# Diffusion trunk on one core: folds issued three weight splits behind, a first weight moved ahead of reloads, background matmuls moved out of a norm

## The chip, the cores and the metric

The kernel runs on one core of a Trainium2 chip. The metric is the device time of one execution, in microseconds, and lower is better. A core has a matrix engine (TensorE, PE in the profile; PEld is its loading of stationary operands), VectorE (DVE), ScalarE (ACT), GpSimd (POOL) and SyncE (SP), which here issues nearly all transfers. Each engine works through its own instructions in the order in which the program was built, and semaphores make one wait for another.

## The reference

One step of a two-layer trunk over 1024 latent and 128 context tokens of width 1024, all in float32. What is computed, cut to what matters:

```python
for i in range(2):
    h = rmsnorm(x, norm_mix_g[i]) * (1 + sc1) + sh1          # sc, sh, gt = silu(c) @ w_mod[i] + b_mod[i]
    x = x + gt1 * (gla_mixer(h) if i == 0 else fourier_mixer(h))
    h = rmsnorm(x, norm_ffn_g[i]) * (1 + sc2) + sh2
    a, g = split(h @ w_up[i])                                 # 2 x 2816 columns
    x = x + gt2 * ((silu(dwconv3(a)) * g) @ w_down[i])        # "ConvGLU"
y = rmsnorm(x, final_norm_g)
```

The first mixer is gated linear attention with 4 heads, whose outputs go through one output product with `gla_w_o`. The second is a Fourier transform over tokens and channel groups, followed by an output product with `fnet_w_o`.

## The kernel before, in words

Every product is made of three matmuls (`mm3`, L94 to L99): each operand is split into a rounded high part, which ACT writes, and the remainder, which DVE or POOL makes by subtraction; the three matmuls are high by high (L97), high by low (L98) and low by high (L99). So each weight goes through a load into a raw tile (`wr`, two buffers), a high part on ACT and a low part on POOL or DVE (`split`, L83, and `weight`, L90; `wh`, six buffers).

The order of the work is not written out: a planner orders each engine's instructions at build time by priority, which is program order, by when operands are ready in its own model, and by free buffers. `tc.high_priority()` moves a block's priority forward, `later(n)` moves it back by n, and `tc.issue_after(ins)` puts the instructions of a block that run on the engine of `ins` behind `ins` in that engine's order, without a wait.

Three places are touched.

**The down product of the ConvGLU** (`ffn`, L979) runs in both layers. It is organised as a one-level fast multiplication: nine steps, the first five of them `a2`, `s1`, `s4`, `a1`, `s2` (`steps`, L1088), each over 11 pairs j of hidden tiles. For each j a step needs the stationary weight of that j, split by `stationary` (L1068: the high part on ACT, L1073, the low part on DVE, L1074), and the moving activations, loaded and split by `moving` (L1077: `hr` loaded by SP, `hh` on ACT, L1083, and `hl` on DVE, L1084, in two pieces of 288 columns; the tiles for them hold two j at a time). Then PE runs 24 matmuls of 288 columns. Steps `s1` and `s4` use sums of weights, which `fold` (L1061) makes in place on DVE (L1064): one fold for each j in `s1`, two in `s4`, each on 128 x 512 elements (the last j has half-width pieces). Before, all folds of a step are placed behind one and the same instruction: `behind` (L1126), the low part that was last traced for the kind of weight that goes before:

```python
if j == 0 and what in ("s1", "s4"):
    behind = made[{"s1": 1, "s4": 2}[what]].ins
```

Step `s2` also folds one weight for each j, after the moving part and with no such edge. The results of a step are added into the residual pages by DVE (L1165).

**The output product of the attention** (`w_out`, L611) multiplies the heads' outputs with `gla_w_o`. Outputs of the first three heads were stored to memory and are loaded again and split by `load_ot` (L604) through the same two raw tiles. For the first two heads `load_ot(0, 1)` stands at L665, before the last head's loop over token groups. `w_out((0, 1), X)` (L675) comes inside that loop, set back by `LV` = 300; it loads its four weights itself, each followed by six blocks of 12 matmuls of 384 columns. Each block ends in an addition on DVE (L624) into one of four pages that `load_x` (L309) has just filled with the residual; even and odd blocks use different pages. A block's result waits in one of three PSUM tiles.

**The Fourier layer and the norm after it.** The modulation vectors of the second ConvGLU are made in small background matmuls (`mod_background`, L150, its matmuls L175 and L186), a generator that `tick` (L193) advances. Its 24 groups are spread by hand: two ticks at each of eight token folds (L1246), two before the time transform of the second pair of channel groups (L1305), two after the output product (L1388), and the rest with `finish()` (L1420) in the midst of the norm of the second ConvGLU, between the variance part of `rstd_steps` (L256) and its broadcast (L273). The ConvGLU's first up-product begins with small weight tiles from `ffn_first_weights` (L864, split by `ffn_split`, L806, here in two halves of 512 columns at L808 and L809), which are traced after that norm, at high priority.

Of the kernel before, what the change touches and what calls it, by code (L numbers as in the profile page):

```python
# [15 lines left out]
F32 = mybir.dt.float32  # L16
# [4 lines left out]
ALU = mybir.AluOpType  # L21
# [10 lines left out]
NCH = 3  # L32
# [13 lines left out]
def trunk(tc, a, o):  # L46
# [43 lines left out]
    def weight(src, n, name, eng=None):  # L90
        with tc.high_priority():
            return split(raw_w(src, n, name), n, name, eng)
# [100 lines left out]
    def tick(n=1, behind=None):  # L193

        for _ in range(n):
            while queue:
                try:
                    with tc.issue_after(behind.ins) if behind else ExitStack():
                        next(queue[0])
                    break  # L200
                except StopIteration:
                    queue.pop(0)

    def finish():
        while queue:
            tick()
# [397 lines left out]
    def load_ot(*hs):  # L604
        for cg, h in ((cg, h) for cg in range(3) for h in hs):
            raw = sb.tile([P, 1032], F32, tag="wr", bufs=2, name="otr")[:, :2 * CH].rearrange("p (d t) -> p d t", d=2)
            nc.sync.dma_start(raw, ot_dram[h][:, :, cols(cg)].rearrange("d p t -> p d t"))
            for d in range(2):
                split_ot(h, d, cg, raw[:, d])

    def w_out(hs, X, after=None):  # L611
        gate = vec(0, 2)
        nk = 2 * len(hs)

        def block(m, ch, whl, mi):
            ps = mm_ps(f"wo{ch}")
            for k in range(nk):
                q = (mi * nk + k) * P
                t = ots[hs[k // 2], k % 2]
                mm3(ps[:, :CH], [w[:, q:q + P] for w in whl],  # L620
                    (t[:, cols(ch)], t[:, T + ch * CH:T + (ch + 1) * CH]), k == 0, k == nk - 1)
            for s, c in parts(ch):
                x = X(m, ch)[:, s]
                V.scalar_tensor_tensor(x, ps[:, s], gate(m, c), x, op0=ALU.mult, op1=ALU.add)  # L624
        if not after:
            for m2 in range(4):
                whl = weight(a["gwo"][0, m2], 1024, f"wo0{m2}")
                for ch in range(NCH):
                    for mi in range(2):
                        block(2 * m2 + mi, ch, whl, mi)  # L630
            return
        ws = []
        for m2 in range(4):
            raw = raw_w(a["gwo"][1, m2], 1024, f"wo1{m2}")
            if m2 < 2:
                pg = page(f"wo1{m2}", F32R)
                whl = pg[:, :1024], pg[:, 1024:2048]
                S.activation(whl[0], raw[:, :1024], AF.Copy)
                G.tensor_tensor(whl[1], raw[:, :1024], whl[0].bitcast(F32), op=ALU.subtract)
                ws.append(whl)  # L640
            else:
                ws.append(split(raw, 1024, f"wo1{m2}"))
        for ch in range(NCH):
            for m in range(KT):
                block(m, ch, ws[m // 2], m % 2)
                feed(X(m, ch), m == 0, span(ch))
                after(m, ch)
# [5 lines left out]
    for h in range(H):  # L653
        with later(LR):
            gla_r(h, pages)
        att = attention(h, qk, pages)
        next(att)
        pages = {}
        if h < 3:
            with later(LQ):  # L660
                qk = gla_qk(h + 1)
                ahead = gla_gates_v(h + 1, pages)
        else:
            finish()
            load_ot(0, 1)  # L665
        for cg in range(3):
            next(att)
            if h < 3:
                with later(LV):
                    next(ahead)  # L670
            elif cg == 0:
                xp, X, Xw = xpages("x1")
                load_x(xp, a["xT"])
                with later(LV):
                    w_out((0, 1), X)  # L675
        for g in (att, ahead):
            for _ in g:
                pass
# [300 lines left out]
    def ffn(l, xp, rs, xd, after, ahead=None, w=None, stages=None):  # L979
# [83 lines left out]
            for (c, xx), (_, yy) in zip(wd[x, j], wd[y, j]):  # L1063
                V.tensor_tensor(xx, *((yy, xx) if reverse else (xx, yy)), op=op)  # L1064

        made = {}

        def stationary(kind, j, wt=None):  # L1068
            if wt is None:
                wt = sb.tile([P, 1032], F32R, tag="wh", bufs=6, name=f"wd{l}")[:, :1024]  # L1070
            for c, x in wd[kind, j]:
                hi, lo = wt[:, c], wt[:, 512:][:, c]
                S.activation(hi, x, AF.Copy)  # L1073
                made[kind] = V.tensor_tensor(lo, x, hi.bitcast(F32), op=ALU.subtract)  # L1074
            return wt

        def moving(name, ss, j):  # L1077
# [31 lines left out]
        for n, (what, name, kind, (mh, th), ss) in enumerate(steps):  # L1109
# [10 lines left out]
            for j in range(NP):  # L1120
                for load, *args in loads.get((n, j), ()):
                    load(*args)
                with tc.high_priority():

                    if j == 0 and what in ("s1", "s4"):
                        behind = made[{"s1": 1, "s4": 2}[what]].ins  # L1126

                    if what == "s1":
                        with tc.issue_after(behind):
                            fold(2, 3, ALU.add, j)  # L1130
                    elif what == "s4":
                        with tc.issue_after(behind):
                            fold(2, 0, ALU.subtract, j)
                            fold(1, 2, ALU.subtract, j)
                    wt = kept.get((what, j))
                    if wt is None or n < 7:
                        wt = stationary(kind, j, wt)
                    hi, lo = moving(name, ss, j)
                    if what == "s2":
                        fold(2, 3, ALU.subtract, j, reverse=True)  # L1140
                held.append((what, ss, wt, hi, lo, what in fresh and j == 0, j == NP - 1))

                if n < len(steps) - 1 or j != NP - 2:
                    for m in range(4):
                        for args in held:
                            products(m, *args)
                    held = []
                if n == 7 and j == 5:
                    norms = after(X, xp, rs, key(1, 0), key(0, 0))
                if n == 8 and j == 5:  # L1150
                    norms = after(X, xp, rs, key(1, 1))
                if n > 6 and j > 4 and j != 6 or n == 8 and j < 5:
                    next(norms, None)
# [110 lines left out]
    for pr_ in range(2):  # L1264
# [36 lines left out]
            i = (g * 2 + typ) * 4 + hl * 2 + half  # L1301
            return pq[i // 6][:, (i % 6) * CH:(i % 6 + 1) * CH]

        if pr_ == 1:
            tick(2)  # L1305
        t2 = weight(a["dft_t"][2][:, :512], 512, f"dt2{pr_}")
        for half in range(2):
            tw = weight(a["dft_t"][half], 1024, f"dt{half}{pr_}")
# [35 lines left out]
    for m in range(KT):  # L1344
# [40 lines left out]
        V.scalar_tensor_tensor(xc, ps2[:, 256:CH], gate(m, 1), xc, op0=ALU.mult, op1=ALU.add)  # L1385
        for ch in range(NCH):
            feed(X(m, ch), m == 0, span(ch))
    tick(2)  # L1388


    def final(X, xp, rs, *keys):
# [23 lines left out]
    xs = dr.tile([KT, P, T], F32, name="xs1")  # L1415
    save_x(xp, xs)
    rs = new_rs()
    norm = rstd_steps(rs, *map(span, range(NCH)))
    next(norm)
    finish()  # L1420
    for _ in norm:
        pass
    ffn(1, xp, rs, xs, final)
    ctx.close()


# [132 lines left out]
```

## Time and profile before

| what | value |
|---|---|
| median of 3 runs (lowest, highest) | 2590.62 us (2589.14, 2591.91) |
| profiled execution | 2588.23 us, its span 2586.4 us |
| mean granted TensorE clock | 0.977 of full speed |
| PE, PEld busy | 2429.6 us (94%), 2332.2 us (90%) |
| DVE, ACT, POOL busy | 1844.4 us (71%), 1090.3 us (42%), 732.9 us (28%) |
| mean transfer rate | 120 GB/s |

The profile shows one execution. Busy time of an engine leaves out waits; idle time is put down to the instruction that ended the wait. A matmul's record is longer than the step from one matmul to the next, as they are pipelined, so the rate of PE is best read from how many matmul records begin in a stretch. A granted clock of 1.00 is 2.4 GHz and one of 0.50 is 1.2 GHz; a value between them is a mix over the stretch.

### The profile page before, as it was taken

What the parts mean: (1) busy time and instruction counts of PE and PEld (TensorE: products, weight loads), DVE (VectorE), ACT (ScalarE), POOL (GpSimd) and SP (SyncE); (2) the same over time, 40 slices, a digit from 0 to 9 for tenths busy, and PEclk for the clock granted to TensorE, in tenths of its full rate; (3) what the DMA queues carried; (4) which work ended last, traced back from release to release, by engine and by line L of the source; (5) the groups of instructions that cost most, each with busy time, mean ns of one, the idle gap of its engine ahead of it and who ended that gap; (6) DMA issues with size and microseconds to landing.
All of it is one profiled execution on the core that took longest, in us unless ns stands there. A gap on an engine that the chain in (4) does not pass through costs nothing. (4 is left out here: it accounts for less than half of the span.)

```text
span 2586.4 us, 46546 instructions
## 1 busy us (share of the span) xinstructions
PE 2429.6 (94%) x18122; PEld 2332.2 (90%) x18122; DVE 1844.4 (71%) x3339; ACT 1090.3 (42%) x2086; POOL 732.9 (28%) x548
## 2 busy tenths in 40 slices
PE   6999999988999999999989998999899999998997
PEld 5998988887999899999989996998899999998997
DVE  7647384666698677777766877287987777787676
ACT  5435343444364233333335564344533333333453
POOL 3435344543103334344100005330144444410000
PEclk9999999998999999999999998999999999999999
DMA  7213222104334443323754347343223232375334
GB/s 261 74 48 93 81 88 79 54 21 145 109 108 126 155 137 99 114 82 101 242 178 134 113 153 214 102 166 134 94 79 115 82 114 82 98 240 176 93 84 126
DMA packets 200972, 309.85 MB, mean 120 GB/s; under 512 B 18288, under 2 KB 142064, under 8 KB 200752
## 3 DMA queue, kind: packets, MB, share of 16 engines
q1 hardware_dynamic: 196528, 302.66, 36.8%
q10 hardware_dynamic: 4224, 4.23, 0.5%
q8 instruction: 142, 2.33, 0.4%
q14 instruction: 78, 0.64, 0.1%
HBM read 233.71 MB, written 73.11 MB: 119 GB/s over the span
## 5 line engine op out<-in xcount | busy, mean ns | idle before, releaser
L98 PE MATMUL pd<-hl,wd 128*128 128x288 f32 x1112 | 331.9, 301 | 28.7 <-DVE hl L1084 28.5
L99 PE MATMUL pd<-hh,wd 128*128 128x288 f32 x1112 | 329.9, 300 | 0.0
L97 PE MATMUL pd<-hh,wd 128*128 128x288 f32 x1112 | 317.6, 299 | 5.5 <-ACT hh L1083 3.2
L98 PEld LDWEIGHTS pd<-hl,wd 128*128 128x128 f32 x1112 | 213.7, 192 | 31.2 <-DVE hl L1084 30.7
L809 POOL TENSOR_TENSOR s<-wa,s 128x512 fp32r<-128x512 f32 x114 | 157.3, 1380 | 278.4 <-ACT s L808 278.4
L1084 DVE TENSOR_TENSOR hl<-hr,hh 128x288 fp32r<-128x288 f32 x308 | 138.3, 454 | 133.8 <-ACT hh L1083 133.5
L1083 ACT ACTIVATE hh<-hr 128x288 fp32r<-128x288 f32 x308 | 133.4, 437 | 233.7 <-PE pd L98 218.8
L97 PEld LDWEIGHTS pd<-hh,wd 128*128 128x128 f32 x1112 | 205.6, 189 | 10.1 <-ACT hh L1083 5.3
L99 PEld LDWEIGHTS pd<-hh,wd 128*128 128x128 f32 x1112 | 213.1, 192 | 0.0
L809 POOL TENSOR_TENSOR a<-wa,a 128x512 fp32r<-128x512 f32 x76 | 100.0, 1316 | 332.4 <-ACT a L808 231.0
L808 ACT ACTIVATE s<-wa 128x512 fp32r<-128x512 f32 x120 | 75.5, 630 | 190.7 <-DVE wa L826 114.7
L977 ACT ACTIVATE hid<-hid 128x576 f32<-128x576 f32 x88 | 60.4, 686 | 157.1 <-DVE hid L972 100.5
L1074 DVE TENSOR_TENSOR wd<-wd,wd 128x512 fp32r<-128x512 f32 (+1 forms) x184 | 116.4, 642 | 9.9 <-ACT wd L1073 4.9
L1073 ACT ACTIVATE wd<-wd 128x512 fp32r<-128x512 f32 (+1 forms) x184 | 104.6, 580 | 26.7 <-DVE wd L1064 14.9
L808 ACT ACTIVATE a<-wa 128x512 fp32r<-128x512 f32 x80 | 50.4, 631 | 142.8 <-PE pa L99 75.9
L1209 POOL TENSOR_TENSOR fn<-fn 128x512 f32<-128x512 f32 x8 | 14.1, 1762 | 330.9 <-ACT wp L728 311.1
L860 DVE TENSOR_TENSOR q<-q,ps 128x288 f32<-128x288 f32 x232 | 98.5, 445 | 11.3 <-PE ps L99 9.7
L535 POOL TENSOR_TENSOR le<-vbr 128x384 f32<-128x384 f32 x72 | 74.3, 1036 | 109.3 <-PE lv L549 93.7
L97 PE MATMUL pa<-fh1x,a 128*128 128x288 f32 x320 | 95.4, 298 | 5.7 <-DVE c L860 3.3
L541 POOL TENSOR_TENSOR le<-le,qk 128x384 f32<-128x384 f32 x72 | 89.4, 1246 | 36.6 <-ACT le L540 35.1
L860 DVE TENSOR_TENSOR c<-q,pa 128x288 f32<-128x288 f32 x80 | 36.1, 451 | 87.7 <-PE pa L99 87.7
L97 PE MATMUL ps<-fh1x,s 128*128 128x288 f32 x320 | 95.2, 298 | 3.0 <-DVE hid L917 3.0
(689 smaller groups left out, 8917.3 us busy)
## 6 DMA issues: line engine op xcount, KB each, us to landing
hr<-hid SPq DMA_DIRECT2D x308, 144.0 KB, 2.2
wm<-in_wmod SPq DMA_DIRECT2D x112, 256.0 KB, 2.8
hid<-hid SPq DMA_DIRECT2D x44, 576.0 KB, 3.9
wa<-in_wup SPq DMA_DIRECT2D x40, 512.0 KB, 3.5
wg<-in_wup SPq DMA_DIRECT2D x40, 512.0 KB, 4.1
hid<-t SPq DMA_DIRECT2D x132, 144.0 KB, 3.3
wd<-in_wdn SPq DMA_DIRECT2D x16, 1024.0 KB, 8.4
wm<-in_wmod SPq DMA_DIRECT2D x96, 128.0 KB, 3.4
```

The lines of the kernel that those rows point to most:

```text
L97: PE.matmul(ps, lhsT=wh, rhs=xh, start=first, stop=False, skip_group_check=skip)
L98: PE.matmul(ps, lhsT=wh, rhs=xl, start=False, stop=False, skip_group_check=skip)
L99: PE.matmul(ps, lhsT=wl, rhs=xh, start=False, stop=last, skip_group_check=skip)
L535: G.tensor_tensor(view(e, 0, [2 * s, nb], [s, 2], [1, s]), ref, view(bb, 0, [2 * s, nb], [CH + s, 2], [1, s]), op=ALU.subtract)
L541: G.tensor_tensor(e[:, 0], e[:, 0], qk[:, base:base + CH], op=ALU.mult)
L808: S.activation(w[name][:, :512], x, AF.Copy)
L809: (eng or G).tensor_tensor(w[name][:, 512:], x, w[name][:, :512].bitcast(F32), op=ALU.subtract)
L860: add.last = V.tensor_tensor(out[:, xs], x[:, xs], ps[s][:, :SUB], op=op)
L1073: S.activation(hi, x, AF.Copy)
L1074: made[kind] = V.tensor_tensor(lo, x, hi.bitcast(F32), op=ALU.subtract)
L1083: S.activation(hi[:, c], raw, AF.Copy)
L1084: V.tensor_tensor(lo[:, c], raw, hi[:, c].bitcast(F32), op=ALU.subtract)
```

## The change

In the down product, `made` becomes a list of all low parts in program order, and the fold for each j is placed behind the low part three before the one about to be traced. In the attention's output product, its first weight is traced before `load_ot(0, 1)`, with the low part on DVE, and `w_out` takes it as `first`. In the Fourier layer the ticks before the time transforms become 2 and 4 for the two pairs; `finish()` stands after the output product in place of two ticks; the norm runs without background matmuls. The first two weights of the second ConvGLU are traced in the output product at m = 5, and two more behind the norm's square root on ACT.

```diff
--- before.py
+++ after.py
@@ -608,7 +608,7 @@
             for d in range(2):
                 split_ot(h, d, cg, raw[:, d])
 
-    def w_out(hs, X, after=None):
+    def w_out(hs, X, after=None, first=None):
         gate = vec(0, 2)
         nk = 2 * len(hs)
 
@@ -624,7 +624,7 @@
                 V.scalar_tensor_tensor(x, ps[:, s], gate(m, c), x, op0=ALU.mult, op1=ALU.add)
         if not after:
             for m2 in range(4):
-                whl = weight(a["gwo"][0, m2], 1024, f"wo0{m2}")
+                whl = weight(a["gwo"][0, m2], 1024, f"wo0{m2}") if m2 else first
                 for ch in range(NCH):
                     for mi in range(2):
                         block(2 * m2 + mi, ch, whl, mi)
@@ -662,6 +662,7 @@
                 ahead = gla_gates_v(h + 1, pages)
         else:
             finish()
+            wo0 = weight(a["gwo"][0, 0], 1024, "wo00", V)
             load_ot(0, 1)
         for cg in range(3):
             next(att)
@@ -672,7 +673,7 @@
                 xp, X, Xw = xpages("x1")
                 load_x(xp, a["xT"])
                 with later(LV):
-                    w_out((0, 1), X)
+                    w_out((0, 1), X, first=wo0)
         for g in (att, ahead):
             for _ in g:
                 pass
@@ -1063,7 +1064,7 @@
             for (c, xx), (_, yy) in zip(wd[x, j], wd[y, j]):
                 V.tensor_tensor(xx, *((yy, xx) if reverse else (xx, yy)), op=op)
 
-        made = {}
+        made = []
 
         def stationary(kind, j, wt=None):
             if wt is None:
@@ -1071,7 +1072,8 @@
             for c, x in wd[kind, j]:
                 hi, lo = wt[:, c], wt[:, 512:][:, c]
                 S.activation(hi, x, AF.Copy)
-                made[kind] = V.tensor_tensor(lo, x, hi.bitcast(F32), op=ALU.subtract)
+                low = V.tensor_tensor(lo, x, hi.bitcast(F32), op=ALU.subtract)
+            made.append(low.ins)
             return wt
 
         def moving(name, ss, j):
@@ -1122,14 +1124,12 @@
                     load(*args)
                 with tc.high_priority():
 
-                    if j == 0 and what in ("s1", "s4"):
-                        behind = made[{"s1": 1, "s4": 2}[what]].ins
 
                     if what == "s1":
-                        with tc.issue_after(behind):
+                        with tc.issue_after(made[-3]):
                             fold(2, 3, ALU.add, j)
                     elif what == "s4":
-                        with tc.issue_after(behind):
+                        with tc.issue_after(made[-3]):
                             fold(2, 0, ALU.subtract, j)
                             fold(1, 2, ALU.subtract, j)
                     wt = kept.get((what, j))
@@ -1301,8 +1301,7 @@
             i = (g * 2 + typ) * 4 + hl * 2 + half
             return pq[i // 6][:, (i % 6) * CH:(i % 6 + 1) * CH]
 
-        if pr_ == 1:
-            tick(2)
+        tick(2 + 2 * pr_)
         t2 = weight(a["dft_t"][2][:, :512], 512, f"dt2{pr_}")
         for half in range(2):
             tw = weight(a["dft_t"][half], 1024, f"dt{half}{pr_}")
@@ -1385,7 +1384,10 @@
         V.scalar_tensor_tensor(xc, ps2[:, 256:CH], gate(m, 1), xc, op0=ALU.mult, op1=ALU.add)
         for ch in range(NCH):
             feed(X(m, ch), m == 0, span(ch))
-    tick(2)
+        if m == 5:
+            first_w = ffn_first_weights(1)
+            ready = [next(first_w), next(first_w)]
+    finish()
 
 
     def final(X, xp, rs, *keys):
@@ -1415,12 +1417,10 @@
     xs = dr.tile([KT, P, T], F32, name="xs1")
     save_x(xp, xs)
     rs = new_rs()
-    norm = rstd_steps(rs, *map(span, range(NCH)))
-    next(norm)
-    finish()
-    for _ in norm:
-        pass
-    ffn(1, xp, rs, xs, final)
+    rstd(rs, *map(span, range(NCH)))
+    with tc.issue_after(rstd.last.ins):
+        ready += [next(first_w), next(first_w)]
+    ffn(1, xp, rs, xs, final, w=chain(ready, first_w))
     ctx.close()
 
 
```

## Rows read from the trace of the kernel before

**Rows 1.** The page's first part: span, busy time by engine.
```profile
span 2586.4 us, 46546 instructions
PE 2429.6 (94%) x18122; PEld 2332.2 (90%) x18122; DVE 1844.4 (71%) x3339; ACT 1090.3 (42%) x2086; POOL 732.9 (28%) x548
```

**Rows 2.** Waits of PE over the span: total us, times, longest.
```profile
PE pd L98 <- DVE hl L1084: 29.0, 7, 10.1
...
PE wo L97 <- ACT wo00h L86: 6.1, 1, 6.1
```

**Rows 3.** Timeline of DVE, the folds of s1 and s4: start, us, instruction.
```profile
1281.19 4.89 DVE L1064 TENSOR_TENSOR wd<-wd,wd 128x512 f32<-128x512 f32 x8
...
1322.62 13.47 DVE L1064 TENSOR_TENSOR wd<-wd,wd 128x512 f32<-128x512 f32 x24
...
2354.69 13.46 DVE L1064 TENSOR_TENSOR wd<-wd,wd 128x512 f32<-128x512 f32 x24
```

**Rows 4.** Stretches: PE, PEld, DVE, ACT, POOL busy; clock, DMA share, GB/s.
```profile
1285.00:1295.00 10.00, 6.32 (x31) 6.09 (x30) 5.95 (x13) 1.30 (x3) 0.00 (x0) 0.66 0.80 259
1300.00:1320.00 20.00, 20.00 (x152) 19.94 (x151) 13.12 (x28) 9.44 (x22) 0.00 (x0) 1.00 0.94 291
1325.00:1345.00 20.00, 9.92 (x58) 9.61 (x57) 15.38 (x30) 3.27 (x8) 0.00 (x0) 0.74 0.20 62
2320.00:2330.00 10.00, 6.52 (x50) 6.37 (x49) 7.35 (x16) 2.60 (x6) 0.00 (x0) 1.00 0.93 301
2355.00:2375.00 20.00, 9.91 (x61) 9.60 (x61) 16.38 (x31) 2.78 (x7) 0.00 (x0) 0.74 0.25 78
```

**Rows 5.** Step s2 of the first layer: the stretch, then DVE's timeline.
```profile
1400.00:1435.00 35.00, 35.00 (x264) 34.93 (x263) 28.91 (x58) 21.58 (x49) 0.00 (x0) 1.00 0.46 138
...
1409.48 0.69 DVE L1064 TENSOR_TENSOR wd<-wd,wd 128x512 f32<-128x512 f32 x1
1410.08 1.22 DVE L715 TENSOR_TENSOR fw<-fw,fw 128x1024 fp32r<-128x1024 f32 x1
```

**Rows 6.** Start of the output product: stretches; timelines of SP, POOL, PE, DVE.
```profile
600.00:610.00 10.00, 5.78 (x21) 5.27 (x22) 8.92 (x9) 4.90 (x8) 8.01 (x4) 0.58 0.78 274
610.00:620.00 10.00, 10.00 (x59) 10.00 (x58) 3.24 (x7) 1.00 (x2) 2.40 (x1) 1.00 1.01 412
...
598.05 1.28 SPq L80 DMA_DIRECT2D wo<-in_gwo  x2
...
608.55 1.45 SPq L309 DMA_DIRECT2D x<-in_xT  x3
...
602.79 2.70 POOL L87 TENSOR_TENSOR wo00l<-wo,wo00h 128x1024 fp32r<-128x1024 f32 x1 [1.12 <-ACT wo00h L86]
...
602.77 0.69 PE L97 MATMUL wo<-ot,wo00h 128*128 128x384 f32 x1 [6.06 <-ACT wo00h L86]
...
605.55 0.69 PE L99 MATMUL wo<-ot,wo00l 128*128 128x384 f32 x1 [1.45 <-POOL wo00l L87]
...
614.64 1.14 DVE L624 SCALAR_TENSOR_TENSOR x<-wo,modT,x 128x384 f32<-128x384 f32 x2 [1.13 <-DMA x<-in_xT]
```

**Rows 7.** The norm of the second ConvGLU: stretch, then timelines of DVE and PE.
```profile
1770.00:1780.00 10.00, 8.70 (x55) 5.79 (x56) 4.09 (x13) 1.16 (x4) 0.00 (x0) 0.62 0.80 267
...
1768.67 0.70 DVE L809 TENSOR_TENSOR a<-w,a 128x512 fp32r<-128x512 f32 x1
...
1776.24 0.56 DVE L270 TENSOR_TENSOR dg<-ident,nw 128x384 f32<-128x384 f32 x1
...
1767.93 1.08 PE L175 MATMUL mods<-wm,cs 128*32 128x128 f32 x32
...
1770.85 0.80 PE L256 MATMUL var<-mean,acc 128*128 128x2 f32 x6 [1.83 <-DVE acc L235]
...
1774.90 2.64 PE L175 MATMUL mods<-wm,cs 128*32 128x128 f32 x22
...
1778.42 4.19 PE L273 MATMUL rstd<-dg,ones 128*128 128x384 f32 x6
```

## The prediction

> **What bounds the kernel now.** I read the busy times first: PE works 94% of the span and no other engine more than 71% [rows 1]. So the time is PE's work plus PE's waits, and a change that leaves PE's work alone can only win or lose in waits and in the clock. Next, what PE waited for: by far the longest total, 29.0 us, is for the low parts `hl` of the down product's moving operand, in 7 waits of up to 10.1 us; one wait of 6.1 us is for the attention output product's first weight [rows 2]. Third, DVE's timeline at those waits: it stands in blocks of folds, 8 in 4.89 us at the entry to `s1` and 24 in 13.47 us at the entry to `s4`, the same in the second layer [rows 3]. All folds of a step hang behind one instruction, so all are ready together and go ahead of the `hl` parts that PE needs; PE has moving tiles for two j only and runs dry.
>
> What this takes is read from PE's rate, since a wait is followed by matmuls at a lower clock. Undisturbed, 152 matmuls begin in 20 us, 7.6 in one, so 0.132 us each. Around the four blocks of folds, 31, 58, 50 and 61 begin where 76, 152, 76 and 152 would, at clocks down to a mean of 0.66 [rows 4]. Missing are 45, 94, 26 and 91, together 256 matmuls of 0.132 us: **33.7 us** is lost, of which at most 29.0 is waiting [rows 2] and the rest, some 4.7 us, is a clock at 1.2 GHz for part of the stretch.
>
> **Part 1, the folds.** Nothing is added or removed: the 12 fold instructions of `s1` and 24 of `s4` stay, at 4.89 / 8 = 0.61 us each [rows 3]. What changes is their place. The fold for j now follows the low part three before its own, so a burst is at most the few for the next j. I count DVE's work for one j of `s4`: two folds 1.22, a low part of 0.6 (same shape as a fold), two `hl` of 0.4, together about 2.6 us, against 24 x 0.132 = 3.2 us on PE. There is room, though little, and the additions of the step before must go into it. The row that is nearest to this is `s2`, which already folds in step: there DVE does one fold of 0.69 for each j and, at every second one, a 1.22 us instruction of the Fourier weights, so as much as two folds for each j, and PE's stretch is full at 264 matmuls in 35 us, 7.5 in one [rows 5]. So the cover for the folds is PE's own 3.2 us for each j, and if DVE falls behind it, each fold costs PE up to its 0.61.
>
> What is late next? The transfers. In the stretch between the two blocks of folds the DMA share is 0.94 while PE is full, and during the blocks it falls to 0.20 to 0.25 [rows 4]. Some of that lull goes: with 5.9 us (45 matmuls) taken out of the 40 us before 1325, a share near 0.9 becomes 0.9 x 40 / 34 = 1.06, so about 2 us of transfers no longer fit in the first layer, and by the same working (26 matmuls, 3.4 us) under 1 us in the second. I take 2.7 us for the two, all of it as waits for moving activations. Part 1: 33.7 - 2.7 = **31.0 us** gained; ends 33.7 (transfers make room, since later weights are not urgent) and 20.3 (one fold of 0.61 stays exposed for each of the 22 j of `s4` in two layers, 13.4 us).
>
> **Part 2, the first weight of the attention's output product.** Now its load stands on SP behind the reloads at 598.05 us, PE idles 6.06 us for the high part and 1.45 us more for the low part, which takes POOL 2.70 us [rows 6]. PE has been idle since 596.7, so 3.3 us go before 600, and in the next 10 us 21 matmuls begin where 59 would, 6.4 us: 9.7 us in all is the upper end. After the change, load and split are done long before, and the low part goes to DVE for about the 1.22 us that an instruction of 128 x 1024 takes there [rows 5]. What is late next is the residual: pages 1 to 3 were issued at 608.55, because SP stood in line for raw tiles, freed only when POOL ends a low part, and DVE had to wait until 614.64 for the first of them [rows 6]. With one weight fewer in that line, the third is freed by POOL one instruction sooner, 2.7 us, so that page lands near 611.9. Six blocks of 12 matmuls (0.17 us each at 59 in 10 us) are 12.2 us and fit between 596.7 and 608.9; the seventh needs a PSUM tile that only the page frees, at about 612.4 with its addition. Before, it began near 602.8 + 1.45 + 12.2 + 2 (low clock) = 618.4. Gain 6.0 us. The lower end counts a cost: the weight keeps two of six split tiles and one raw tile from the last head's own weights; if those come late by a wait like the one removed, 6.1 us, nothing is left. I take **6.0**, ends 9.7 and 0. On PE the shift stays, since its next stretch is full [rows 6].
>
> **Part 3, the norm and what was moved out of it.** Out of the norm go 64 records of background matmuls, from 32 at 1767.93 to 22 at 1774.90 [rows 7]. The first 32 lie under PE's wait of 1.83 us for the accumulated squares and cost nothing. The last 22 end at 1777.5, though the diagonal for the broadcast was ready at 1776.24 + 0.56 = 1776.8; the broadcast starts at 1778.42: 1.6 us. Those between the variance matmuls take about 1 us. Two low parts of the up-product's weights, 2 x 0.60 us at 1768.67, stand on DVE ahead of the last additions; after the change they go sooner, or, behind the square root, into DVE's idle time in the norm: 1.2 us. Together 3.8 us. Against it, half of the background records now run in the Fourier stage, where PE is the bound: 32 at 1.08 us [rows 7]. The loads of their weights move with them on SP, and the first two up-product weights, two loads and two splits, go ahead of the last output weights in the same six tiles; DVE and SP are not full there, and one product has about the time of 50 matmuls of 0.17 us to refill two tiles, so I count nothing, and one load and split, 3 us, at the lower end. Sum **2.4**, ends 3.8 and -2.
>
> A row speaks against counting on more here: the granted clock was already 0.62 with the background matmuls in place, and each broadcast of two records takes 1.4 us [rows 7]. The Trainium skill, "Perfetto Trace Analysis", section "Matmul Optimizations", says that the engine scales its power with utilization, so "it's important that matmuls execute back-to-back in batches"; by that rule emptier PE time in the norm would be paid for in the matmuls after it. The trace agrees that idle PE time can lower the clock (0.66 in one stretch, though 1.00 in another with a wait [rows 4]); that a few background matmuls keep it up it does not show.
>
> **Sum.** 31.0 + 6.0 + 2.4 = 39.4 us less than the profiled execution's 2588.23, so 2548.8. The median of the runs shown is 2.4 us above that execution; against it the forecast is 2590.62 - 39.4 = **2551 us**, rounded.
>
> **Rivals.**
> (a) Folds stay partly exposed: DVE falls behind in `s4`, where step evictions add to the 2.6 us. For it: only 0.6 us of slack for each j. Against: `s2`. 13.4 us less gain instead of 2.7: 2562.
> (b) The output product gains nothing, because the last head's weights or the residual pages come as late as PE comes early. For: SP's line. Against: no wait for those weights is among PE's longest [rows 2]. 2557.
> (c) The norm is no faster: PE is emptier in it, and the up-product starts at 1.2 GHz, as matmuls did after the waits in the down product; with 2.4 us lost there (half of the 4.7 us that the clock took at the folds, an estimate), part 3 is zero: 2553. This is what the rule cited in part 3 would do here.
> (d) The change does not do what it says: the edge orders issue only, and the planner could still put many folds in a row. Only parts 2 and 3: 2582.
> (e) Slower than before: head-of-line waiting on DVE. A fold now stands between low parts; a low part waits for ACT's high part, that for a split tile which PE frees, and the next `hl` waits behind all of it. If every j of `s1` exposes a low part and a fold (1.2 us) and every j of `s4` a low part and two folds (1.8 us), 22 each, PE loses 66 us against 42 gained elsewhere (33.7 + 6 + 2.4): 2590.6 + 24 = 2615. It decides from 42 / 44 = 0.96 us lost for each j. Against it: `s2` has this very order and no loss.
>
> **How the numbers follow.** Chances: forecast 0.70, (a) 0.10, (b) 0.08, (c) 0.05, (d) 0.02, (e) 0.05, of which 0.02 near the point where it cancels the gain. The range reaches from all three upper ends, 33.7 + 9.7 + 3.8 = 47 us, 2543, and a little beyond for order that falls out better elsewhere, 2541, to (a) with part 2 at half: 2566. It leaves out (d) and (e) and some spread. Within 0.2% (5 us, about what a measurement of this kernel can tell from no change): 0.02; slower 0.03; faster 0.95.
>
> **What would show it.** In the profile after: DVE's timeline has no row of more than 4 folds, and PE's wait for `hl` falls from 29.0 us to under 4; if not, part 1 is wrong, and if waits for `hh` or for the load of `hr` grow instead, the transfers are the reason. PE's first output block starts before 598 with no wait for `wo00h`, and a wait for the residual appears near 609. The broadcast starts 3 to 4 us sooner after the last output matmul, with no L175 between. A drop of less than 20 us, or a new wait of PE above 10 us, would make the prediction wrong.

## The result and the profile after

The changed kernel takes 2563.6 us in the median of 4 runs (2561.6 to 2565.3), beside 2591.3 us for the kernel before (2589.1 to 2595.1). The ratio is 0.9891, 95% interval [0.9874, 0.9908], so 28.2 us are gained. A second measurement (e5 below), beside other runs of the kernel before, gave 0.9870 [0.9847, 0.9892], 33.8 us. The forecast was 39.4 us less, 2551 us: the range held the result, but 6 to 11 us of the gain that was forecast did not come. The profiled execution took 2562.35 us.

From the page of the changed kernel, its span and the line of busy times, which answer to [rows 1]:

```profile
span 2560.5 us, 46534 instructions
...
PE 2418.9 (94%) x18122; PEld 2323.7 (91%) x18122; DVE 1843.0 (72%) x3340; ACT 1091.0 (43%) x2086; POOL 728.0 (28%) x547
```

PE has 11 us less of busy time and 26 us less of span; it is still the bound. PE's waits over the span (total us, times, longest), which answer to [rows 2]:

```profile
PE ov L577 <- DVE os L575: 17.6, 12, 8.5
...
PE pd L98 <- DVE hl L1086: 5.3, 5, 1.8
...
PE rstd L273 <- DVE dg L270: 5.0, 2, 3.2
```

The wait for `hl` fell from 29.0 to 5.3 us (1.6 us of it, waits of 0.5 to 0.6 us, stood in the kernel before as well), and the 6.1 us for `wo00h` are gone. But the wait for `os`, the summed squares of the last head's output norm, was 11.7 us in 12 waits of at most 2.6 us before; now one of them alone takes 8.5 us.

**The folds.** The changed kernel's timeline of DVE and PE around the folds (start, us, instruction; the idle time before it in brackets), to be held against [rows 3]:

```profile
1327.77 0.69 DVE L1065 TENSOR_TENSOR wd<-wd,wd 128x512 f32<-128x512 f32 x1
...
1342.27 0.50 DVE L1165 SCALAR_TENSOR_TENSOR xd<-pd,modT,xd 128x288 f32<-128x288 f32 x1
...
1348.18 2.03 DVE L1065 TENSOR_TENSOR wd<-wd,wd 128x256 f32<-128x256 f32 x5
...
1350.12 1.19 DVE L1086 TENSOR_TENSOR hl<-hr,hh 128x288 fp32r<-128x288 f32 x3
...
1350.63 0.40 PE L98 MATMUL pd<-hl,wd 128*128 128x288 f32 x1 [1.82 <-DVE hl L1086]
...
2366.36 0.40 PE L98 MATMUL pd<-hl,wd 128*128 128x288 f32 x1 [1.83 <-DVE hl L1086]
```

The blocks of 8 and 24 are gone: nearly every fold is a row of one among the `hl`. One bunch is left in each layer, at the last folds of `s4`: three `hl` stand behind five folds (four half-width ones and a full one), which DVE only reaches after the evictions of `s1` (L1165), and PE waits 1.82 and 1.83 us for them. DVE folds several j ahead of PE: when this bunch begins, PE is only 9 us into `s4`. In the same way the two blocks of the kernel before, which the prediction puts at the entries to `s1` and `s4`, ran while PE was 21 us into `a2` and 18 us into `s1`. The stretches of the changed kernel, columns as in [rows 4]:

```profile
1280.00:1290.00 10.00, 10.00 (x78) 10.00 (x77) 8.61 (x19) 4.06 (x10) 0.00 (x0) 1.00 0.91 281
...
1340.00:1360.00 20.00, 18.18 (x131) 17.36 (x130) 15.24 (x36) 7.91 (x19) 0.00 (x0) 1.00 0.30 83
...
2305.00:2315.00 10.00, 10.00 (x77) 10.00 (x76) 6.79 (x13) 3.90 (x9) 0.00 (x0) 1.00 0.99 302
...
2355.00:2375.00 20.00, 18.17 (x119) 17.31 (x119) 14.47 (x34) 6.36 (x17) 0.00 (x0) 0.91 0.28 77
```

Where the block of 8 had stood, PE is full (78 and 77 matmuls in 10 us). Around the last folds of `s4`, 131 and 119 matmuls begin where 152 would.

**The output product.** From the kernel before, ACT's timeline at the last head's output norm:

```profile
589.78 0.49 ACT L573 ACTIVATE os<-o 128x384 f32<-128x384 f32 x1 [1.79 <-PE o L570]
...
592.48 0.49 ACT L574 ACTIVATE os<-o 128x384 f32<-128x384 f32 x1 [0.28 <-PE o L570]
```

The changed kernel's timelines of ACT, DVE, POOL, SP and PE around 600 us, to be held against these and [rows 6]:

```profile
594.68 0.49 ACT L573 ACTIVATE os<-o 128x384 f32<-128x384 f32 x1
...
602.77 1.06 ACT L86 ACTIVATE wo01h<-wo 128x1024 fp32r<-128x1024 f32 x1
...
603.73 0.51 ACT L601 ACTIVATE ot<-otr 128x384 fp32r<-128x384 f32 x1
...
604.97 0.47 ACT L574 ACTIVATE os<-o 128x384 f32<-128x384 f32 x1
...
604.27 2.40 DVE L602 TENSOR_TENSOR ot<-otr,ot 128x384 fp32r<-128x384 f32 x1 [1.76 <-ACT ot L601]
...
608.33 0.55 DVE L575 TENSOR_TENSOR os<-os,os 128x384 f32<-128x384 f32 x1
...
611.84 1.14 DVE L582 SCALAR_TENSOR_TENSOR o<-o,gng,os 128x384 f32<-128x384 f32 x2 [2.50 <-ACT os L579]
...
603.90 2.35 POOL L87 TENSOR_TENSOR wo01l<-wo,wo01h 128x1024 fp32r<-128x1024 f32 x1 [5.24 <-ACT wo01h L86]
...
607.15 1.51 SPq L309 DMA_DIRECT2D x<-in_xT  x3
...
609.02 1.62 PE L577 MATMUL ov<-os,ones 128*128 128x384 f32 x2 [8.47 <-DVE os L575]
...
613.57 0.69 PE L97 MATMUL wo<-ot,wo00h 128*128 128x384 f32 x1 [2.93 <-DVE x L624]
```

The first block of `wo00` now ran at 583.06, in the gaps of the last head. But on ACT the second square of `os` came at 604.97, ten microseconds after the first, behind the high part of `wo01` and splits of reloads; before, the two were 2.7 us apart. DVE, which has splits of head outputs to do first, adds them at 608.33, and PE, which must issue `ov` before its next output block, stands 8.47 us. Then it waits 2.93 us more for an addition into the residual. Here the transfer was not what held it: the trace has the first residual page landed at 605.70, and on DVE the addition stands behind the last head's output (L582 at 611.84), which needs `ov` itself. The other three pages were issued at 607.15.

**The norm.** The changed kernel's timelines of PE and DVE, against [rows 7]:

```profile
1760.39 2.14 PE L256 MATMUL var<-mean,acc 128*128 128x2 f32 x18 [2.06 <-DVE acc L235]
...
1765.70 4.06 PE L273 MATMUL rstd<-dg,ones 128*128 128x384 f32 x6 [3.17 <-DVE dg L270]
...
1763.39 0.69 DVE L810 TENSOR_TENSOR a<-w,a 128x512 fp32r<-128x512 f32 x1
...
1764.00 0.68 DVE L810 TENSOR_TENSOR g<-w,g 128x512 fp32r<-128x512 f32 x1
...
1764.60 0.16 DVE L265 TENSOR_TENSOR nw<-nw 128x9 f32<-128x9 f32 x1
```

No background matmul is left between the variance and the broadcast. But two low parts of the up-product's weights now stand on DVE in the middle of the norm's own chain, 1.2 us from 1763.39 to 1764.60, and PE waits 3.17 us for the diagonal.

### The profile page after: what moved, and what is told of

The parts are those of the page before. It is cut to its first block, busy times and chain, and to the rows that moved or that the text cites. A ratio compares the mean times of both kernels' runs of the same rounds, so it can differ in the third digit from the quotient of the medians.

```text
span 2560.5 us, 46534 instructions
## 1 busy us (share of the span) xinstructions
PE 2418.9 (94%) x18122; PEld 2323.7 (91%) x18122; DVE 1843.0 (72%) x3340; ACT 1091.0 (43%) x2086; POOL 728.0 (28%) x547
## 5 line engine op out<-in xcount | busy, mean ns | idle before, releaser
L1086 DVE TENSOR_TENSOR hl<-hr,hh 128x288 fp32r<-128x288 f32 x308 | 138.4, 455 | 107.4 <-ACT hh L1085 106.8
L97 PE MATMUL ps<-fh0t,s 128*128 128x288 f32 x320 | 97.2, 304 | 1.4 <-DVE c L861 1.4
```

The lines of the kernel that those rows point to most:

```text
L97: PE.matmul(ps, lhsT=wh, rhs=xh, start=first, stop=False, skip_group_check=skip)
L1086: V.tensor_tensor(lo[:, c], raw, hi[:, c].bitcast(F32), op=ALU.subtract)
```

## The experiments

Each timed kernel was compared with the kernel before on its own chip. To see where a difference lies I also took lengths of stages from PE's records, from the first matmul of one product to the first of the next (us):

| stage | before | e1 | e2 | e3 | after | e5 | e6 | e7 |
|---|---|---|---|---|---|---|---|---|
| start to weight `wr31` of the last head | 564.6 | 569.3 | 569.6 | 568.3 | 567.6 | 567.0 | 567.1 | 564.7 |
| `wr31` to the second output product | 105.0 | 106.9 | 106.8 | 106.8 | 106.3 | 106.1 | 95.8 | 95.4 |
| down product, first three steps, first layer | 128.2 | 112.0 | 127.5 | 128.5 | 110.6 | 112.2 | 112.1 | 112.1 |
| down product, first three steps, second layer | 122.5 | 111.4 | 125.2 | 124.5 | 111.1 | 109.9 | 110.4 | 110.9 |
| end of the first down product to `st` | 43.2 | 39.2 | 42.7 | 41.4 | 39.9 | 39.2 | 38.9 | 41.0 |
| time transforms and Fourier output product | 129.3 | 129.8 | 129.3 | 133.8 | 134.8 | 134.3 | 133.9 | 129.5 |
| last output matmul to the broadcast | 10.8 | 11.1 | 11.0 | 7.7 | 7.7 | 7.7 | 7.7 | 10.3 |

Each column is one profiled execution. The first row is work that no edit touches (but for the split of the one moved weight), and differs by 5 us between executions: single traces can't be compared by their ends. Rows of one stage can, within limits: where e1 and e3 have the code of the kernel before, the second row still differs from it by 1.9 us.

**The parts one by one.** e1 is the kernel before with the folds in step alone (in part; the line is the same for `s1` and `s4`):

```diff
-                        with tc.issue_after(behind):
+                        with tc.issue_after(made[-3]):
```

> The kernel before with the folds in step and nothing else. Theory (folds carry the gain, some 6.8 us of the 33.7 stay): about 28 us less than before, ratio 0.989, PE's wait for the low parts hl about 5 us instead of 29, the longest near 1.8 us, at the last folds of s4. Forecast as written: 31 us less, ratio 0.988. Rival (the parts help each other, and the folds alone gain clearly less): under 22 us, ratio above 0.9915.

Measured: 0.9866 [0.9852, 0.9881], 34.8 us less, 30.9 to 38.4 by the interval. From the waits of e1:

```profile
PE pd L98 <- DVE hl L1085: 5.6, 6, 1.8
...
PE s L97 <- DVE pq L1330: 5.1, 3, 2.4
```

The waits for `hl` are as the theory has them, and the gain is larger than its 28 us. In the table the down product gives 28.7 us of it, against the mean of the three kernels with the old folds (128.03 to 112.04 and 124.07 to 111.40), and the stage behind it 3 us. The second line is used at e3.

e2 has the first weight alone (`wo0 = weight(...)` ahead of `load_ot`, and `first=wo0`):

> The kernel before with the output product's first weight ahead of the head outputs and nothing else. Theory (PE's wait only moves from that weight to the sum of squares of the last head, which ACT now reaches behind other splits): no difference, within 2 us, ratio 0.999 to 1.001; PE waits some 8 us for os where it waited 6.1 us for the weight. Forecast as written: 6 us less, ratio 0.9977. Rival (the weight's tiles delay the last head): 3 us or more slower, ratio above 1.001.

Measured: 1.0004 [0.9992, 1.0016], no difference. PE waits 8.81 us for `os` and 2.93 us for the residual, where e1 waits 5.98 us and 1.53 us for the weight. From `wr31` to the second output product both take the same 106.8 us. The theory holds: the wait moved.

e3 has the third part alone:

> The kernel before with the ticks moved, the norm without background matmuls and its weights sooner, and nothing else. Theory (3 us gained in the norm, half of it paid back in the Fourier stage): 1 to 2 us less, ratio 0.9992 to 0.9996, so no difference that this can tell in the time alone; in the trace the stretch from the last output matmul to the broadcast is 3 us shorter and the Fourier stage before it 1 to 5 us longer. Forecast as written: 2.4 us less, ratio 0.9991. Rival (the Fourier stage pays more than the norm gains): 2 us or more slower.

Measured: 1.0010 [1.0002, 1.0019], 2.6 us slower: the rival. The norm is 3.1 us shorter, as expected, but the time transforms and the output product ahead of it are 4.5 us longer. Timelines of PE and DVE of e3 in the time transforms:

```profile
1696.36 0.38 PE L97 MATMUL s<-dt01h,dat 128*128 128x256 f32 x1 [1.34 <-DVE pq L1330]
...
1699.81 0.38 PE L97 MATMUL s<-dt11h,dat 128*128 128x256 f32 x1 [1.16 <-DVE n L1325]
...
1703.72 0.38 PE L97 MATMUL s<-dt11h,dat 128*128 128x256 f32 x1 [2.66 <-DVE pq L1330]
...
1700.91 1.56 DVE L1350 SCALAR_TENSOR_TENSOR fsum<-fo,row 128x512 f32<-128x512 f32 x1 [1.16 <-DMA fo<-in_fwo]
...
1703.11 1.49 DVE L1330 TENSOR_TENSOR pq<-s,pq 128x384 fp32r<-128x384 f32 x3
```

Where the kernel before has one wait of 2.68 us here, e3 has three, 5.2 us in all. Before the last of them DVE works the sums of the output product's weights (`fsum`) first, waits for their load, and only then makes the low part `pq` that the transform's tile waits for. The 64 records of background matmuls that moved here take 2.2 us at the rate of [rows 7] (32 take 1.08). The other 2.3 us can't simply be put down to the waits: e1, which has the old third part, waits 5.1 us for `pq` as well, and its stage is only 0.5 us longer than before (129.8 us). What the kernel before doesn't lose by waiting it loses by the clock, 0.85 and 0.81 of full speed in the two stretches of 10 us from 1680, where e1 has 1.00 from 1669 to 1689. e9 separates the two.

**Behind the first weight.** e4 asks whether the late squares are the wall (a wall is here an operand that holds PE up, whatever else is ready):

```diff
-            S.activation(sq0, po[0][:, :CH], AF.Square)
-            S.activation(sq1, po[1][:, :CH], AF.Square)
-            V.tensor_tensor(sq0, sq0, sq1, op=ALU.add)
+            with tc.high_priority() if h == 3 else ExitStack():
+                S.activation(sq0, po[0][:, :CH], AF.Square)
+                S.activation(sq1, po[1][:, :CH], AF.Square)
+                V.tensor_tensor(sq0, sq0, sq1, op=ALU.add)
```

> The changed kernel with the two squares and their sum of the last head's output norm at high priority. Theory (the late square on ACT is what PE stands for at 600 us): the wait of 8.5 us for os falls under 3 us, and the time is 3 to 8 us below the changed kernel, ratio to before 0.986 to 0.988. Rival (the residual pages are a wall at the same place, whatever comes before): the wait for os goes, the wait for the residual x grows by as much, and the time is that of the changed kernel within 2 us, ratio 0.989 to 0.990.

Measured: 0.9880 [0.9867, 0.9894], no clear difference to the changed kernel. Timelines of DVE, PE and SP of e4:

```profile
598.12 0.55 DVE L575 TENSOR_TENSOR os<-os,os 128x384 f32<-128x384 f32 x1
...
612.73 0.69 PE L474 MATMUL kt<-ident,ke 128*128 128x128 f32 x2 [11.35 <-POOL ke L471]
...
604.29 2.08 SPq L309 DMA_DIRECT2D x<-in_xT  x4
...
611.74 1.13 DVE L624 SCALAR_TENSOR_TENSOR x<-wo,modT,x 128x384 f32<-128x384 f32 x2
...
613.40 0.62 DVE L624 SCALAR_TENSOR_TENSOR x<-wo,modT,x 128x384 f32<-128x384 f32 x1 [0.53 <-DMA x<-in_xT]
```

`os` is added ten microseconds sooner and its wait is gone, but PE now stands 11.35 us for the next thing in its order, the transposes of the next group: DVE begins their operand `ke` at 610.34, behind the last head's output, whose `ov` PE had begun at 600.57 and ACT took up at 604.58. The residual would have held PE about as long: three output blocks had been made by then and filled the three PSUM tiles, and the additions that free them begin at 611.74, as the residual was only issued from 604.29 on and its first page landed at 610.50. So the rival was right on the time, though PE's wait is not for the residual: there are two more walls at the same place.

e5 is the changed kernel once more, e6 takes e4 and loads the residual ahead of the last head's loop, e7 takes e6 without the third part:

```diff
             load_ot(0, 1)
+            xp, X, Xw = xpages("x1"); load_x(xp, a["xT"])
         for cg in range(3):
...
-                xp, X, Xw = xpages("x1")
-                load_x(xp, a["xT"])
```

> The changed kernel itself, beside the next three on one chip. If the parts add up as measured one by one (0.9866, 1.0004 and 1.0010), its ratio to before is 0.988; the first result was 0.9891.

> The changed kernel with the squares of the last head first and the residual pages of the output product loaded ahead of that head's loop. Theory (after the first weight the next walls are the squares and then the residual, and PE stands only because both come late): no wait of PE over 4 us between 580 and 640 us, and 6 to 11 us less than the changed kernel, ratio to it 0.9957 to 0.9977. Rival (the transfers of the residual, 4.6 MB, only push back the reloads of the head outputs, and PE waits for these): within 2 us of the changed kernel.

> The kernel of the run before this one without the change's third part: ticks and norm as in the kernel before. Theory (the third part costs more in the Fourier stage than it gains in the norm, 1.0010 alone): 2 to 3 us less than with it, and 8 to 14 us less than the changed kernel. Rival (the third part gains its 2.4 us once the rest is fast): 2 us more than with it.

Measured: e5 0.9870 [0.9847, 0.9892], 2563.3 us (2560.6 to 2568.3); e6 0.9835 [0.9811, 0.9858], 2556.8 us (2548.6 to 2560.5); e7 0.9820 [0.9803, 0.9837], 2552.0 us (2549.0 to 2554.4). e6 is 6.5 us below the changed kernel, e7 11.4 us, and the runs of neither overlap with those of e5, though e6 clears them by 0.1 us only. What makes it firm is that all six kernels with the residual sooner (e6, e7, e9 to e12) have ratios of 0.982 to 0.9835, and the changed kernel, e4 and e8 0.987 to 0.989. The residual sooner without the squares first was not tried. The stage from `wr31` on is 10 us shorter in both. Timelines of SP, DVE, PE and POOL of e7:

```profile
588.69 0.37 SPq L309 DMA_DIRECT2D x<-in_xT  x1
...
594.40 0.61 DVE L624 SCALAR_TENSOR_TENSOR x<-wo,modT,x 128x384 f32<-128x384 f32 x1
...
605.28 0.44 PE L97 MATMUL wo<-ot,wo01h 128*128 128x384 f32 x1 [1.91 <-ACT wo01h L86]
...
607.82 0.44 PE L99 MATMUL wo<-ot,wo01l 128*128 128x384 f32 x1 [1.75 <-POOL wo01l L87]
...
605.31 2.46 POOL L87 TENSOR_TENSOR wo01l<-wo,wo01h 128x1024 fp32r<-128x1024 f32 x1 [3.36 <-ACT wo01h L86]
...
605.47 2.72 DVE L546 TENSOR_TENSOR le<-le,qk 128x384 f32<-128x384 f32 x1
```

The first page of the residual is issued 11 us sooner than `wo01`, its first addition runs at 594.40, and nothing of PE's stands for `os`, the transposes or the residual; what is left is 1.91 and 1.75 us for the second weight. The third part's price comes out a second time in the table: 4.4 us in the Fourier stage against 2.6 us in the norm. The intervals of e6 and e7 overlap, so the times alone don't show it.

**What is left.** e8 sets the folds of `s4` one low part further back in the changed kernel (`made[-4]`):

> The changed kernel with the folds of s4 placed behind the low part four before their own instead of three. Theory (what stays of the folds is one bunch behind the step evictions at the end of s4): the waits of 1.8 us for hl at the end of s4 fall under 1 us in both layers, 2 to 4 us less than the changed kernel. Rival (the bunch only moves to the entry of s4, where four folds now stand in a row): within 1 us, with a new wait for hl near the entry.

Measured: 0.9871 [0.9848, 0.9894], the time of e5. Timelines of DVE and PE of e8:

```profile
1307.68 1.96 DVE L1065 TENSOR_TENSOR wd<-wd,wd 128x256 f32<-128x256 f32 x4
...
1345.27 0.40 PE L98 MATMUL pd<-hl,wd 128*128 128x288 f32 x1 [0.64 <-DVE hl L1086]
...
2325.12 0.40 PE L98 MATMUL pd<-hl,wd 128*128 128x288 f32 x1 [0.68 <-DVE hl L1086]
...
2363.18 0.40 PE L98 MATMUL pd<-hl,wd 128*128 128x288 f32 x1 [0.64 <-DVE hl L1086]
```

The waits of 1.8 us are down to 0.64 us, and the first three steps take 111.0 and 109.2 us, 1.8 us less than in e5. `s4` alone takes 36.7 us in both layers, where e5 has 37.9 and 38.0. At the first folds of `s4` there are now four in a row, two of them half-width. The wait of 0.68 us near there in the second layer is not theirs: the four begin at 2325.59, after it, and e5 and e7 wait 0.28 and 1.30 us at the same place. So the bunch is the cause of the waits of 1.8 us, as the theory has it; 2 us is less than the time can tell.

e9 takes e6 and sets six single ticks into the Fourier output product instead of ahead of the transforms:

```diff
-        tick(2 + 2 * pr_)
+        if pr_ == 1: tick(2)
...
+        if m < 6: tick()
```

> The kernel with the residual sooner (with the change's third part), but the ticks ahead of the time transforms as in the kernel before, and six single ticks in the Fourier output product, one after each of its first six blocks. Theory (what the third part loses in the Fourier stage is 64 more matmuls, 2.2 us, and 2.7 us of waits that they cause there by coming between the transforms and their results): the time transforms fall back from 63.5 to 59.6 us, the output product grows from 66.2 to about 68.5 us, the norm stays at 7.7 us; with the pages unchanged some 2 us less than with the residual sooner alone, ratio to before 0.982 to 0.983. Rival (the cost is the matmuls alone, wherever they stand): no difference to it, 0.9835.

Measured: 0.9835 [0.9819, 0.9851], the ratio of e6: the rival. The transforms are back at 59.4 us (63.3 in e6) and the waits there at those of the kernel before, as expected. But the output product, counted to the start of its last matmul, grows from 70.4 to 73.1 us, so only 1.3 us came of it, and the time doesn't show them. The whole stage is still 3.3 us longer than in the kernel before (132.6 against 129.3): most of the third part's price in this stage is the matmuls themselves, where PE is the bound, and more than the 2.2 us that 64 of them take in the norm.

The last three build on e7: e10 with the low parts of `wo01` to `wo03` on DVE, e11 with `made[-4]` in `s4`, e12 with both:

```diff
-                whl = weight(a["gwo"][0, m2], 1024, f"wo0{m2}") if m2 else first
+                whl = weight(a["gwo"][0, m2], 1024, f"wo0{m2}", V) if m2 else first
```

> The kernel with the residual sooner and the old norm, but the low parts of all four first weights of the output product on DVE instead of POOL. Theory (DVE instructions of 0.55 us take 2.5 us while POOL subtracts a weight, so moving the weight to DVE costs it no more than it loses now, and the low part is ready 1.2 us sooner): the wait of 1.75 us for the low part falls under 0.8 us, and the splits of the head outputs beside it take 0.5 us each; 1 to 2 us less than the old norm alone (0.982), which the time alone can hardly tell. Rival (DVE is late with the additions that free PSUM): PE waits for x instead, no gain.

> The kernel with the residual sooner and the old norm, with the folds of s4 four low parts behind. Theory: the three steps of the down product from the first to the entry of the fourth take 110.5 and 109.3 us instead of 112.1 and 110.6, 2 to 3 us less in all, ratio to before about 0.981. Rival (no gain that lasts): 0.982.

> Both of the two edits before this one on the kernel with the residual sooner and the old norm. If each brings its part, 3 to 5 us less than 2552 us, ratio to before about 0.980 to 0.981; if neither lasts, 0.982.

Measured: e10 0.9830 [0.9812, 0.9849], e11 0.9820 [0.9803, 0.9838], e12 0.9831 [0.9811, 0.9851]: none differs from e7. e11's first three steps take 109.5 and 109.2 us, 4 us less than e7's, and its median of 2549.7 us is the lowest of all, but its interval is that of e7. Timelines of DVE, ACT and PE of e10:

```profile
606.04 0.55 DVE L546 TENSOR_TENSOR le<-le,qk 128x384 f32<-128x384 f32 x1
...
606.97 1.22 DVE L87 TENSOR_TENSOR wo01l<-wo,wo01h 128x1024 fp32r<-128x1024 f32 x1
...
605.06 1.06 ACT L86 ACTIVATE wo01h<-wo 128x1024 fp32r<-128x1024 f32 x1 [3.66 <-DMA wo<-in_gwo]
...
606.17 0.45 PE L97 MATMUL wo<-ot,wo01h 128*128 128x384 f32 x1 [2.23 <-DVE ke L469]
...
608.25 0.44 PE L99 MATMUL wo<-ot,wo01l 128*128 128x384 f32 x1 [1.28 <-DVE wo01l L87]
```

DVE does a low part in 1.22 us and its neighbours keep their 0.55 us. PE still waits 2.23 us before `wo01`, put down to an instruction of DVE, and 1.28 us for the low part: that weight is bound by its load, for which ACT stood 3.66 us until 605.06. Of all kernels tried e7 and e11 have the lowest ratio, 47 us below the kernel before, with e10 and e12 inside their intervals.

## Why the prediction was right, and where its sizes were off

The direction and the cause were right: PE ran dry behind blocks of folds, and folding in step gives the whole gain. One by one the parts gave 34.8 - 1.0 - 2.6 = 31.2 us (e1, e2, e3), which lies between the two results for all of them together, 28.2 and 33.8. So the parts add up as far as the intervals tell. That the sum came within its range owes something to luck: parts 2 and 3 were forecast to gain 8.4 us and lost 3.6, while part 1 gained 3.8 us more than forecast. The forecast of 39.4 splits as follows.

**Part 1, forecast 31.0, measured 34.8 [30.9, 38.4].** The step "33.7 - 2.7" had a wrong second term. I counted 2.7 us for transfers that no longer fit. But PE's wait for `hh` is 5.1 us in 6 waits in both kernels, and none for a load came; what is left is mostly 21 + 33 = 54 missing matmuls in the two stretches of `s4`, 7.1 us at 0.132 us. They stand around the bunch of last folds behind the step evictions; loosening it (e8) brings `s4` from 37.9 to 36.7 us, where 35.25 is undisturbed, so nearly half of the loss is shown to be the bunch and the rest stays open. That was rival (a)'s place, though much smaller than its 13.4 us. The first term was too small as well: against three undisturbed steps of 35.25 us in each layer (the third step of the kernel before) the three steps are 128.03 + 124.07 - 211.5 = 40.6 us too long with the old folds, since I counted nothing of what was lost outside my four stretches, and by the same working still 11.9 us in e1. The difference, 28.7 us, came near the forecast of 31.0 with both terms undersized, which is luck. Three further microseconds come from the stage behind the first down product (42.4 us on average with the old folds, 38.9 to 39.9 in e1, after, e5 and e6). It holds none of the moved instructions, and e7, e8, e9 and e10 with 41.0 to 41.6 don't have all of it; its cause stays open.

**Part 2, forecast 6.0, measured -1.0 [-4.2, 2.1].** Rival (b)'s result, by a way that it didn't name. The step that failed is "what is late next is the residual": I followed SP and POOL, and took ACT, and with it the last head's output norm, as unmoved. The planner builds each engine's whole order anew when one weight is traced elsewhere. On ACT the second square went behind `wo01h` and the reloads; DVE and PE followed. Even without that (e4) PE could not have gone on before about 611.7, when the first addition into the residual ran. That this is near my 611.9 is luck: I had that for the second page, and took the first as there in time. So I let six blocks run ahead, three of them freed by the first page; but the first additions came at 612.90 in the changed kernel and 611.74 in e4, and until then PE could fill three PSUM tiles and no more. With the walls taken away (e6, e7) the stage gives 10 us, the 9.7 of my upper end.

**Part 3, forecast 2.4, measured -2.6 [-4.9, -0.5].** In the norm the forecast was 3.8 and the trace shows 3.1: the low parts that I had going "into DVE's idle time" stand in the chain for 1.2 us. The step that failed is "32 at 1.08 us" for the Fourier stage: all 64 records moved ahead of the transforms, not half of them, and there they cost more than their 2.2 us. The stage is 4.5 us longer in e3; e9, where the waits between transforms and results are those of the kernel before, still keeps 3.3 us of that. So the larger error is the price of a background matmul where PE is the bound, taken from a row in which PE waited anyway; the waits, which I gave no price, are the smaller one. Why a record costs more there stays open.

**Rival (c), the clock.** It found no support. From the first up-product matmul to the next product it takes 54.7 us before and 54.6 after. The Trainium skill, "Perfetto Trace Analysis", section "Matmul Optimizations", asks for matmuls back to back because the engine scales its power with use. Here an emptier norm was not paid for in the matmuls after it; the granted clock is 1.00 in the 10 us in which the up-product starts, from 1783 before and from 1770 after. Rivals (d) and (e) fell with e1.

Of the signs that I gave, most came as written: first output block before 598 and no wait for `wo00h`, the broadcast 3.1 us sooner, no L175 in between, and a drop above 20 us. Three didn't: a row of five folds is left, the wait for `hl` stopped at 5.3 us, not under 4 (3.65 us of it at that row; the 1.6 us that were there before I had not taken off), and the wait for an addition into the residual came at 613.6, not near 609, and by way of `os`, not of the transfer. A new wait of 8.5 us came just under the 10 us that I had set.

## What to carry to other kernels

Instructions that hang behind one release become one block: spread them over the loop at the pace of their use, and look at the places where evictions come on top. When the longest wait at a place is taken away, list everything that PE will issue after it and when each operand is ready; here several walls stood within 15 us (the weight, the squares, the transposes, the residual), and taking the first away gave nothing until the others went. Filler work taken out of one stage has to go where the engine truly waits: in or ahead of a stage that PE bounds it costs at least its full length (3.3 us for 64 records in e9, 3 us gained in the norm). And a sum of waits is no price by itself: e1 waits 2.4 us longer than the kernel before in the same transforms, and the stage is 0.5 us longer.

## What the runs showed of the hardware

DVE instructions that take 0.55 us took 2.4 and 2.7 us while POOL subtracted a weight (604.27 beside 603.90 in the changed kernel, 605.47 beside 605.31 in e7). With that subtraction moved to DVE (e10) they took 0.55 us, and the subtraction itself 1.22 instead of 2.46 us. The Trainium skill, "SBUF — State Buffer", section "SBUF: two separate sides", says that DVE and GpSimd share a port pair as an exclusive lock held for a whole instruction, also against a DVE operation with two inputs in SBUF. The trace agrees: both slow DVE instructions end 0.4 us after POOL's (606.67 after 606.25, 608.19 after 607.77).
